# Matrix product with layer norm: another row order in the opening's row tiles, and their pieces of A loaded one by one

## The chip, the cores and the metric

The kernel runs on one core of a Trainium2 chip. The metric is the device time of one execution in microseconds; of several runs the median counts. Five engines work side by side, each with its own queue of instructions: TensorE (PE, matmuls and transposes; PEld is its loading of weights), VectorE (DVE), ScalarE (ACT), GpSimd (POOL) and SyncE (SP, which here issues most of the transfers). Sixteen DMA engines move data between the chip's memory and the on-chip buffers.

## The reference

```python
def setup_inputs():
    m, k, n = 2048, 2048, 2048
    return {
        "a": np.random.randn(m, k).astype(np.float32),
        "b": np.random.randn(k, n).astype(np.float32),
        "gamma": np.random.randn(n).astype(np.float32),
        "beta": np.random.randn(n).astype(np.float32),
        "eps": np.float32(1e-5),
    }

def reference(a, b, gamma, beta, eps):
    x = np.matmul(a, b)
    mean = np.mean(x, axis=-1, keepdims=True)
    var = np.var(x, axis=-1, keepdims=True)
    normalized = (x - mean) / np.sqrt(var + eps)
    return (gamma * normalized + beta).astype(np.float32)
```

Every row of the product is normalised by itself, so rows may be computed in any order.

## The kernel before

A, B and the output are 2048 x 2048 in float32. The rows of A are cut into 16 row tiles of 128, the contraction into 16 steps of 128 (`kt`), the columns of the output into 4 quarters of 512 (`q`). A quarter of a row tile is 16 matmuls into one PSUM bank, 1024 matmuls in all. The operands are float16: B is cast once and stays on the chip (`b16`), each row tile of A is cast and transposed, so that the contraction lies on the partitions (`at`).

Two stages follow each other.

*The opening* computes the first R = 5 row tiles together while B is still coming in, since each piece of B then serves five row tiles. A comes in column pieces of 512 (`c` = 0 to 3). For `c` = 0 each row tile's piece is a load of its own of 256 KB (`load_a1`, line 182), in the order of `arrivals` (line 163): A0, B0, A1, A2, A3, B1, B2, A4, B3. For `c` = 1 to 3 `load_pair` loads the pieces of row tiles 0 and 1, then 2 and 3, by one transfer of 512 KB each (`load_a2`, line 188) and that of row tile 4 alone (`load_a1`). All of them, and those of B (`load_b1`, `load_b2`), are issued by SP in program order, into six staging buffers (`stg`); a load waits until the casts have emptied its buffer. VectorE casts each arrived piece (lines 186, 194, 199, 205). PE transposes the pieces of A for `c` = 0 to 2 (`turn`, line 252, by hand-set spots among the matmuls) and ScalarE copies them to `at`; for `c` = 3 the transpose is a DMA (`turn_last`, line 258, in SP's queue). Until the first pieces are there, PE runs filler matmuls (line 245). The opening's parts of sums are set aside in `xs` and added up later on VectorE (`put_aside`, `add_part`, `add_rest`).

*The rest* runs row tiles 5 to 15 one after the other, with B on the chip. GpSimd loads a whole row tile with the cast in the transfer (`load_row`, line 345), and SP transposes it by DMA (`turn_ahead`, line 351), two row tiles ahead.

A row tile that is complete is normalised in two halves (`queue_norm`: `centre`, `scale`), each of which ends with one store of two quarters (`store`, line 121, issued by SP). These pieces are worked off one at a time between the quarters of later row tiles. The last row tile has an ending of its own (`finish_row`) with four stores of one quarter.

In all of this partition p of row tile i holds row 128 i + p of A and of the output.

Of the kernel before, what the change touches and what calls it, by code (L numbers as in the profile page):

```python
# [16 lines left out]
def kernel(  # L17
# [9 lines left out]
    nc = tc.nc  # L27
    P = 128
# [9 lines left out]
    KW = KC * P  # L38
    n_kc = n_kt // KC
    R = 5  # L40
# [28 lines left out]
    xs = [None] * n_mt  # L69
# [39 lines left out]
    def centre(i, q, mv):  # L109
        qs = ds(q * NB, NB)  # L110
        nc.vector.scalar_tensor_tensor(  # L111
            xs[i][:, qs], xs[i][:, qs], mv[:, 0:1], gamma_b[:, qs],
            AluOp.subtract, AluOp.mult)

    def scale(i, q, rstd):
        qs = ds(q * NB, NB)
        nc.vector.scalar_tensor_tensor(  # L117
            xs[i][:, qs], xs[i][:, qs], rstd, beta_b[:, qs],
            AluOp.mult, AluOp.add)

    def store(i, q0, nq):
        s = ds(q0 * NB, nq * NB)
        nc.sync.dma_start(out[ts(i, P), s], xs[i][:, s])

    def inv(i, sq):
        rstd = stat.tile([P, 1], FP32, tag="rstd", name=f"rstd{i}")
        nc.vector.reciprocal(rstd, sq)
        return rstd

    def queue_norm(i, mv, sq):  # L130

        got = {}

        def piece(q0):
            def run():
                centre(i, q0, mv)
                centre(i, q0 + 1, mv)
                if q0 == 0:
                    got["rstd"] = inv(i, sq)
                scale(i, q0, got["rstd"])  # L140
                scale(i, q0 + 1, got["rstd"])
                store(i, q0, 2)
            return run

        backlog.extend(piece(q) for q in range(0, n_nb, 2))

    def drain(n):
# [7 lines left out]
        out=ident, in_=ident, compare_op=AluOp.not_equal, fill=1.0,  # L155
# [7 lines left out]
    arrivals = [("a", 0), ("b", 0)] + [("a", i) for i in range(1, R - 1)]  # L163
    arrivals += [("b", 1), ("b", 2), ("a", R - 1), ("b", 3)]

    a16_of = {}
    fresh = {"st": 0}
    held = {}

    def half_stage():  # L170
        n = fresh["st"]
        if n % 2 == 0:
            held["st"] = stg.tile([P, 2, NB], FP32, tag="st", name=f"st{n // 2}")
        fresh["st"] += 1
        return held["st"][:, n % 2, :]

    def a16_room(i, c):
        if i % KC == 0:
            held["a"] = a16p.tile([P, KC, KW], FP16, tag="a16", name=f"a16s{i}_{c}")
        a16_of[i, c] = held["a"][:, i % KC, :]  # L180

    def load_a1(i, c):
        st = half_stage()
        nc.sync.dma_start(st, a[ts(i, P), ts(c, KW)])  # L184
        a16_room(i, c)
        nc.vector.tensor_copy(a16_of[i, c], st)  # L186

    def load_a2(i, c):
        st = stg.tile([P, 2, NB], FP32, tag="st", name=f"sta{i}_{c}")
        nc.sync.dma_start(  # L190
            st, a[ds(i * P, 2 * P), ts(c, KW)].rearrange("(t p) k -> p t k", p=P))
        for m in (0, 1):
            a16_room(i + m, c)
        nc.vector.tensor_copy(held["a"][:, ds(i % KC, 2), :], st)  # L194
# [6 lines left out]
    def load_b2(k, q, cast=nc.vector.tensor_copy):  # L201
        st = stg.tile([P, 2, NB], FP32, tag="st", name=f"stb{q}_{k}")
        nc.sync.dma_start(
            st, b[ds(k * P, 2 * P), ds(q * NB, NB)].rearrange("(t p) n -> p t n", p=P))
        cast(b16[:, k:k + 2, ds(q * NB, NB)], st)  # L205
        return st
# [3 lines left out]
    def load_pair(j, c):  # L210
        if len(pairs[j]) == 2:
            load_a2(pairs[j][0], c)
        else:
            load_a1(pairs[j][0], c)

    for what in arrivals:
        (load_a1(what[1], 0) if what[0] == "a" else load_b1(what[1]))
# [139 lines left out]
    for n, (k, q) in enumerate(later):  # L357
        for i in {0: (0,), 1: (1,), 2: (2,), 4: (3, 4)}.get(n, ()):
            turn_last(i)
        st = load_b2(k, q, nc.scalar.copy)  # L360
# [39 lines left out]
    def finish_row(i):  # L400
# [35 lines left out]
        rstd = inv(i, mv[:, 1:2])  # L436
        scale(i, 3, rstd)
        store(i, 3, 1)
        centre(i, 0, mv)
        for q in (1, 2):  # L440
            for h in (0, 1):
                nc.scalar.activation(  # L442
                    half(q, h), y_ps[q, h], ActFn.Copy, scale=rstd)
            store(i, q, 1)
            if q == 1:
                scale(i, 0, rstd)
                store(i, 0, 1)
# [69 lines left out]
```

## Time and profile before

| | us |
|---|---|
| median of 3 runs (lowest, highest) | 244.88 (243.92, 245.12) |
| the profiled execution, its own time | 245.38 |
| its span, first to last instruction | 242.9 |
| PE busy in the span | 234.3 |
| VectorE, ScalarE, GpSimd busy | 171.2, 65.9, 12.7 |
| matmuls of the product (line 85) busy | 223.0 |

| loads and stores | number, KB each | median us from issue to landing |
|---|---|---|
| A, one row tile's piece (`st`) | 8 x 256 | 6.5 |
| A, two row tiles' pieces (`sta`) | 6 x 512 | 6.5 |
| B, opening, one step (`st`) | 4 x 256 | 6.6 |
| B, two steps (`stb`) | 30 x 512 | 6.8 |
| stores of two quarters | 30 x 512 | 3.3 |

Times of the trace are counted from the start of the span. An engine's busy time says what it did, not what the end waited for; for that the chain of waits is read, which goes back from the last instruction to whatever released each step. The granted clock of TensorE was 0.994 over the span.

### The profile page before, as it was taken

The page shows a single profiled execution, that of the slowest core. Times are in us where ns is not written, and L with a number is a line of the kernel's source. Part 1 is how long each engine was busy: PE and PEld are TensorE (multiplying, and loading weights), DVE is VectorE, ACT ScalarE, POOL GpSimd, SP SyncE. Part 2 cuts the span into 40 slices and gives each one's busy share as a digit, 9 for nine tenths or more (in the row PEclk, how much of TensorE's full clock was granted, in tenths as well). Part 3 has the DMA queues.
Part 4 walks back from the last instruction along what each step waited for, and adds up shares of the span by engine and source line. Part 5 has one row for each costly group of instructions (what it writes and reads, how often), then busy time and mean ns, then how long its engine had stood idle before and what let it go on. Part 6 is the DMA issues. An engine that isn't in the chain of part 4 may idle for free.

```text
span 242.9 us, 2971 instructions
## 1 busy us (share of the span) xinstructions
PE 234.3 (96%) x1117; PEld 107.2 (44%) x1117; DVE 171.2 (70%) x300; ACT 65.9 (27%) x115; POOL 12.7 (5%) x20
## 2 busy tenths in 40 slices
PE   7899999999999999999999999999999999999992
PEld 2344554344444444444444444444444444444441
DVE  1543554625449998999999999998758292846761
ACT  2376444065750013020201103022111121212132
POOL 0000000000120001000000000005400000000000
PEclk9999999999999999999999999999999999999997
DMA  5999999999979999749899978988907235130405
GB/s 101 391 387 387 385 366 300 275 356 386 385 153 198 350 224 169 233 154 205 248 200 233 254 166 292 245 202 199 260 33 170 89 112 150 47 126 1 173 0 173
DMA packets 43909, 53.28 MB, mean 219 GB/s; under 512 B 27124, under 2 KB 27124, under 8 KB 43640
## 3 DMA queue, kind: packets, MB, share of 16 engines
q1 hardware_dynamic: 42312, 47.34, 62.7%
q0 software_dynamic: 1584, 5.77, 14.5%
q8 instruction: 8, 0.13, 0.2%
q14 instruction: 5, 0.04, 0.0%
HBM read 35.67 MB, written 16.78 MB: 216 GB/s over the span
## 4 chain that ended last, share of the span: by engine, by line
PE 93%; DMA 2%; DVE 1%; ACT 1%; SPq 0%; issue 0%; DVEq 0%
PE acc L85 91%; DMA st<-in_a_dram 2%; PE tps L252 1%; ACT x L442 1%; DVE x L268 1%; DVE bnst L407 0%; PE y L430 0%; DVE a16s L186 0%; PE warm L245 0%; SPq L198 0%; SPq L184 0%; PE ms_ps L425 0%; ACT mv_last L423 0%; DVE mv_last L422 0%; ACT lead L426 0%
## 5 line engine op out<-in xcount | busy, mean ns | idle before, releaser
L85 PE MATMUL acc<-b,at 128*128 128x512 f16 x1024 | 223.0, 379 | 1.5 <-DVE b L199 1.0
L85 PEld LDWEIGHTS <-at 128*128 128x128 f16 x1024 | 99.7, 98 | 120.5 <-issue 1.2
L96 DVE BATCH_NORM_STATS2 bnst<-x 128x6 f32<-128x512 f32 x43 | 29.5, 689 | 23.4 <-ACT x L95 23.4
L117 DVE SCALAR_TENSOR_TENSOR x<-x,rstd,beta_b 128x512 f32<-128x512 f32 x62 | 43.9, 748 | 0.6
L111 DVE SCALAR_TENSOR_TENSOR x<-x,mv,gamma_b 128x512 f32<-128x512 f32 x60 | 43.1, 760 | 0.0
L95 ACT COPY x<-acc 128x512 f32<-128x512 f32 x43 | 24.5, 585 | 66.9 <-PE acc L85 66.7
L272 DVE TENSOR_TENSOR x<-acc,x 128x512 f32<-128x512 f32 x20 | 13.6, 678 | 13.4 <-PE acc L85 13.4
L106 ACT ACTIVATE sq<-ve 128x1 f32<-128x1 f32 x15 | 3.0, 203 | 65.8 <-DVE ve L104 65.8
L205 DVE CAST b<-stb 128x1024 f16<-128x1024 f32 x16 | 11.1, 694 | 13.1 <-DMA stb<-in_b_dram 13.1
L205 ACT CAST b<-stb 128x1024 f16<-128x1024 f32 x14 | 14.6, 1045 | 16.6 <-DMA stb<-in_b_dram 16.6
L273 DVE BATCH_NORM_STATS2 bnst<-x 128x6 f32<-128x512 f32 x20 | 13.9, 694 | 0.7
L264 ACT COPY x<-acc 128x512 f32<-128x512 f32 x20 | 10.2, 610 | 5.7 <-PE acc L85 5.7
L254 ACT COPY at<-tps 128x512 f16<-128x512 f16 (+1 forms) x11 | 8.0, 741 | 13.1 <-PE tps L252 12.9
L345 POOL DMA_DIRECT2D a<-in_a_dram x11 | 6.0, 545 | 92.8 <-DMA at<-a 92.0
L245 PE MATMUL warm<-zeros 128*128 128x512 f16 x19 | 6.5, 476 | 1.2 <-DVE zeros L152 1.2
L186 DVE CAST a16s<-st 128x512 f16<-128x512 f32 x8 | 3.4, 428 | 5.7 <-DMA st<-in_a_dram 5.6
L194 DVE CAST a16s<-sta 128x1024 f16<-128x1024 f32 x6 | 4.2, 694 | 4.1 <-DMA sta<-in_a_dram 4.1
L391 POOL TENSOR_SCALAR gb<-gb 1x1024 f32<-1x1024 f32 x2 | 5.8, 2917 | 0.0
L252 PE MATMUL tps<-ident,a16s 128*128 128x128 f16 x60 | 5.2, 220 | 0.6 <-DVE a16s L186 0.6
L252 PEld LDWEIGHTS <-a16s 128*128 128x128 f16 x60 | 3.9, 98 | 3.9 <-DVE a16s L186 2.2
L102 DVE BATCH_NORM_AGGREGATE mv<-bnst 128x2 f32<-128x24 f32 x15 | 4.0, 264 | 0.5
L245 PEld LDWEIGHTS <-zeros 128*128 128x128 f16 x19 | 2.1, 118 | 4.4 <-issue 2.9
(33 smaller groups left out, 26.3 us busy)
## 6 DMA issues: line engine op xcount, KB each, us to landing
stb<-in_b_dram SPq DMA_DIRECT2D x30, 512.0 KB, 6.8
out_dram<-x SPq DMA_DIRECT2D x30, 512.0 KB, 3.3
a<-in_a_dram POOLq DMA_DIRECT2D x11, 512.0 KB, 6.2
sta<-in_a_dram SPq DMA_DIRECT2D x6, 512.0 KB, 6.5
st<-in_a_dram SPq DMA_DIRECT2D x8, 256.0 KB, 6.5
st<-in_b_dram SPq DMA_DIRECT2D x4, 256.0 KB, 6.6
gamma_b<-in_gamma_dram SPq DMA_DIRECT2D x1, 1024.0 KB, 5.5
beta_b<-in_beta_dram SPq DMA_DIRECT2D x1, 1024.0 KB, 8.3
```

The costliest lines, as they stand in the source:

```text
L85: nc.tensor.matmul(acc[i, q], at(i)[:, kt, :], b16[:, kt, ds(q * NB, NB)], start=first, stop=last,)
L95: nc.scalar.copy(xs[i][:, qs], acc[i, q])
L96: nc.vector.bn_stats(bnst[i][:, q, :], xs[i][:, qs])
L111: nc.vector.scalar_tensor_tensor(xs[i][:, qs], xs[i][:, qs], mv[:, 0:1], gamma_b[:, qs], AluOp.subtract, AluOp.mult)
L117: nc.vector.scalar_tensor_tensor(xs[i][:, qs], xs[i][:, qs], rstd, beta_b[:, qs], AluOp.mult, AluOp.add)
L205: cast(b16[:, k:k + 2, ds(q * NB, NB)], st)
L245: nc.tensor.matmul(warm if to is None else to, zeros[:, 0:P], zeros, start=True, stop=True)
L252: nc.tensor.transpose(t_ps[:, m, j, :], a16_of[i, c][:, ts(j, P)], ident)
L254: nc.scalar.copy(pair[i0 // 2][:, ds(i0 % 2, n), ds(c * KC, KC), :], t_ps)
L264: nc.scalar.copy(xs[p][:, ds(q * NB, NB)], acc.pop((p, q)))
L272: nc.vector.tensor_tensor(xs[p][:, qs], acc[p, q], xs[p][:, qs], AluOp.add)
L273: nc.vector.bn_stats(bnst[p][:, q, :], xs[p][:, qs])
```

## The change

Row tiles 0 to 4 keep their 128 rows, but these lie on the partitions in another order: partition 8e + j holds row e + 16j (e from 0 to 15, j from 0 to 7). The new function `spread` is this view of a row tile in memory. The loads of A in the opening (`load_a1`, `load_a2`) read through it and the stores of row tiles 0 to 4 write through it, so that each row ends up where it belongs. B and row tiles 5 to 15 keep their order.

`load_a2` issues two transfers of 256 KB, one for each row tile, in place of one of 512 KB; the cast behind them is still one for both. Row tile 0 is stored by four transfers of one quarter in place of two of two quarters.

```diff
     def store(i, q0, nq):
         s = ds(q0 * NB, nq * NB)
-        nc.sync.dma_start(out[ts(i, P), s], xs[i][:, s])
+        nc.sync.dma_start(spread(out, i, s) if i < R else out[ts(i, P), s], xs[i][:, s])
...
                 scale(i, q0 + 1, got["rstd"])
-                store(i, q0, 2)
+                for q, nq in ((q0, 1), (q0 + 1, 1)) if i == 0 else ((q0, 2),):
+                    store(i, q, nq)
...
+    def spread(x, i, cols):
+        return x[ts(i, P), cols].rearrange("(j e) n -> e j n", e=16)
...
     def load_a1(i, c):
         st = half_stage()
-        nc.sync.dma_start(st, a[ts(i, P), ts(c, KW)])
+        nc.sync.dma_start(st, spread(a, i, ts(c, KW)))
...
     def load_a2(i, c):
         st = stg.tile([P, 2, NB], FP32, tag="st", name=f"sta{i}_{c}")
-        nc.sync.dma_start(
-            st, a[ds(i * P, 2 * P), ts(c, KW)].rearrange("(t p) k -> p t k", p=P))
+        for m in (0, 1):
+            nc.sync.dma_start(st[:, m, :], spread(a, i + m, ts(c, KW)))
```

## The prediction

> **What bounds the kernel now.** I read the chain that ended last first, then the busy times, then the opening by stretches of time, then the two queues that the change touches. The page's chain of waits (section 4: shares of the span by engine, then by line):
>
> ```profile
> PE 93%; DMA 2%; DVE 1%; ACT 1%; SPq 0%; issue 0%; DVEq 0%
> ```
>
> Nine tenths of the span is one unbroken run of matmuls (line 85). The same chain in order of time (start us, duration us, what) shows where it is not PE:
>
> ```profile
> 1.66 6.00 DMA st<-in_a_dram
> 7.66 0.02 issue
> 7.69 0.44 DVE a16s L186
> ...
> 12.31 12.73 PE acc L85 x59
> ...
> 48.17 185.79 PE acc L85 x860
> ```
>
> From 1.66 to 7.66 us the end is set by a load of A (row tile 1, column piece 0). From 12.31 on PE never waits for a load; its one pause, around 47 us, is for PSUM banks that VectorE empties. So the change can move the end in two ways: let the first tiles land at another time, or make a later piece of A so late that PE waits for it. The opening by stretches (start:end and length in us, then busy us and counts of PE, PEld, DVE, ACT, POOL, the granted clock, the DMA engines' busy share, GB/s):
>
> ```profile
> 0.00:3.00 3.00, 1.81 (x5) 0.71 (x6) 0.35 (x2) 1.28 (x1) 0.49 (x5) 1.00 0.22 70
> 3.00:6.00 3.00, 2.44 (x12) 0.91 (x11) 0.43 (x1) 0.16 (x1) 0.00 (x0) 1.00 0.80 126
> 6.00:9.00 3.00, 1.87 (x14) 0.68 (x12) 1.28 (x3) 0.82 (x2) 0.00 (x0) 1.00 1.05 395
> ...
> 12.00:36.00 24.00, 24.00 (x146) 12.15 (x145) 11.41 (x18) 13.24 (x22) 0.00 (x0) 1.00 1.05 384
> 36.00:48.00 12.00, 11.73 (x54) 5.15 (x53) 6.36 (x10) 2.54 (x5) 0.00 (x0) 1.00 1.08 282
> ```
>
> This is the table to look at twice. Between 3 and 6 us the sixteen DMA engines are 80% busy and move 126 GB/s; from 6 us on, just as busy, they move 385 to 395. Whatever they do in the ramp, it is not moving bytes at their pace, though five loads had been issued by then. Last, VectorE's casts (start us, duration us, engine, line, operation; in brackets the idle time before and what ended it), which give the arrival of each piece:
>
> ```profile
> 4.92 0.43 DVE L186 CAST a16s<-st 128x512 f16<-128x512 f32 x1 [3.71 <-DMA st<-in_a_dram]
> 7.01 0.43 DVE L199 CAST b<-st 128x512 f16<-128x512 f32 x1 [1.67 <-DMA st<-in_b_dram]
> 7.69 0.43 DVE L186 CAST a16s<-st 128x512 f16<-128x512 f32 x1 [0.25 <-DMA st<-in_a_dram]
> 8.36 0.43 DVE L186 CAST a16s<-st 128x512 f16<-128x512 f32 x1 [0.25 <-DMA st<-in_a_dram]
> ```
>
> The first piece of B lands 2.09 us after the first of A (7.01 - 4.92); every later 256 KB piece lands 0.67 to 0.68 us after the one before. 0.68 us for 262,144 B is 386 GB/s, the pace of the full stream.
>
> **The change, part by part.**
>
> 1. *The matmuls, transposes, casts and statistics* keep their number and shapes: the row order inside a row tile is only a name for a partition, and rows 0 to 4 are stored back through the same view. Cost 0.
>
> 2. *Two loads for one in `load_a2`*, six times. On SP each extra issue costs 0.46 us (three of line 184 back to back take 1.37 us; line 190 alone takes 0.37), 6 x 0.46 = 2.8 us of SP. It lies beside the stream: a piece of A lands a median 6.5 us after its issue because it queues behind others, and from 11.5 to 36 us SP issues loads of 0.37 us about every 1.4 us and otherwise waits for staging room. If that cover were gone, the second half of each pair, and behind it the next load of B in SP's order, would be 0.46 us late, and the cast in line 194 with it. On the DMA engines the split costs what the cadence shows: 256 KB pieces come every 0.68 us, 512 KB pieces (casts at 17.14, 18.50, 19.85) every 1.36; 2 x 0.68 - 1.36 = 0. The cast now needs two landings; one more semaphore step of 0.017 us (what such a step takes on SP before line 203) x 6 = 0.1 us on VectorE, which stands idle 0.67 us before each of these casts. Queued behind that cast on VectorE are the next casts of B, and PE waits for those only if they lose more than the slack given below. I take the middle, 0.05 us; bounds 0 and 0.1. [...]
>
> 3. *Row 0 stored by four transfers instead of two.* Two more issues of about 0.4 us on SP near 97 us. SP waits 103.4 us in all there for VectorE (line 117), up to 10.2 at once, and behind these stores stands one transpose of A at 107.74 for a row tile that PE reaches later. Cost 0; without that idle time 0.8 us for this transpose.
>
> 4. *The stores of rows 0 to 4 through the view.* Today ten transfers, median 3.3 us to landing, from 97 to about 130 us, while PE runs its 185.79 us without a wait and the last store is row 15's, which is not touched. Cost 0, with over 80 us of cover.
>
> 5. *The order in which A's rows are read*, the only part with a price. No row shows a read in the new order, so I bound it. Best end: the ramp goes away. From 3 to 6 us (388 - 126) x 3.00 = 786 KB were not moved (388 GB/s is the rate from 12 to 15 us in a finer table), and 786 KB at 388 GB/s is 2.03 us. Every us of it moves A1's landing at 7.66, and with it the whole chain, since behind it PE and the load stream shift together. Gain at most 2.03 us. Worst end: the new order is read more slowly than the stream. The nearest row of a slower stream is 282 GB/s (36 to 48 us, where other work shares the engines): 0.93 us a piece instead of 0.68, worked out below to 2.8 us of loss. Between them I take the share of the ramp that is A's: of the six loads issued first (A0, B0, A1, A2, A3, B1) four are A's, 4/6 x 2.03 = 1.35 us. I lean to the gain because the steady stream already runs with all engines out of step and at its pace, so the new order has little to lose there, whereas the ramp, where all engines begin together at rows a fixed distance apart, is the place where the order can matter.
>
> [...]
>
> Sum: -1.35 + 0.05 = -1.3 us. The profiled execution took 245.38 us (span 242.9 and 2.5 around it), 0.5 over the median of the runs, 244.88. It would take 244.1, the median 243.6.
>
> **The rivals.**
>
> *A. The order does not matter: 244.9 us.* The ramp is then the engines' or the memory's way of starting, whatever is read. For it: the ramp hits B0 as well (its cast begins at 7.01), which is read as before. The steady stream cannot gain: at 384 to 395 GB/s A and B come at one pace. Against it: the DMA engines count as busy in the ramp. The same time follows if the new view is turned into the same reads.
>
> *B. The new order is slower than the stream: about 246.9 us.* Each engine then steps 128 KB from row to row instead of 8 KB if the view is cut as its name says. Place: the transposes of row tiles 2 and 3, third column piece. Their cast runs from 30.20 to 30.89, PE begins them at 31.63: a slack of 0.74 us, the smallest in the opening. Up to there 14 pieces of A (5 + 5 + 4) have come through a stream without gaps, so this decides from 0.74 / 14 = 0.053 us a piece, 8% slower. At 282 GB/s it is 14 x 0.254 - 0.74 = 2.8 us; halfway between there and a loss just over 1.2 us, 2.0. For it: the stream has no gaps from 6 to 36 us, so every lost ns adds up. Against it: between 12 and 36 us loads of A and of B, in single rows or in pairs of rows 1 MB apart, come at one and the same pace, so the stream there seems not to ask in what order rows are read.
>
> **How the numbers follow.** This kernel's runs lie 0.5% apart, so 0.5% (1.22 us) is about what can be told from no change: 243.66 to 246.10 is "same". The forecast (a gain from 0.3 to 2.0 us) gets 0.52, of which 0.38 is over 1.22 us and 0.14 under. Rival A gets 0.18, all within. Rival B gets 0.30, of which 0.27 is over 1.22 us. Faster 0.38, same 0.14 + 0.18 + 0.03 = 0.35, slower 0.27. The range begins at 242.6 (the whole ramp, 2.03, and 0.25 of scatter) and goes into rival B up to 246.6, leaving out some 0.15 there and 0.04 below. The forecast's own range is 242.6 to 244.6.
>
> **What would show it.** The forecast holds if the cast of B0 begins before 6.5 us, that of A1 before 6.8, and the stretch from 3 to 6 us moves well over 126 GB/s, with 384 GB/s kept from 12 to 36 us. Rival A: the same arrival times within 0.2 us. Rival B: casts of single pieces of A more than 0.73 us apart, and PE waiting for line 194 near 31 us. Parts 2 to 4 are wrong if PE waits for a cast while 384 GB/s still hold, or if the transposes of A after 97 us come late. The prediction as a whole fails if the ramp gets longer, for B0 too: then the order matters with the other sign.

## The result and the profile after

The changed kernel takes 255.66 us (median of 6 runs, 253.73 to 256.76) against 244.61 us before (6 runs). The ratio is 1.0458, 95% interval 1.0426 to 1.049: slower by some 11 us, where 1.3 us of gain was forecast. The profiled execution was the fastest of the six, 253.73 us with a span of 251.8; a second one (e15_again) took 254.52 with 252.5.

The opening by the same stretches of time as before (start:end, length, busy us of PE, PEld, DVE, ACT, POOL, granted clock, busy share of the DMA engines, GB/s):

```profile
0.00:3.00 3.00, 1.81 (x5) 0.71 (x6) 0.35 (x2) 1.28 (x1) 0.50 (x5) 1.00 0.19 44
3.00:6.00 3.00, 2.68 (x11) 0.95 (x10) 0.43 (x1) 0.00 (x0) 0.00 (x0) 1.00 0.74 160
6.00:9.00 3.00, 2.57 (x13) 0.80 (x10) 1.20 (x3) 0.95 (x2) 0.00 (x0) 1.00 1.09 296
...
12.00:36.00 24.00, 21.11 (x120) 10.09 (x117) 8.92 (x14) 11.84 (x20) 0.00 (x0) 1.00 1.06 312
```

The ramp is hardly touched (160 GB/s instead of 126). What broke is the stream behind it: from 12 to 36 us the engines are as busy as before (1.06 against 1.05) and move 312 GB/s instead of 384, and PE, which had been busy all 24 us, is busy for 21.11. Engines as busy that move less mean slower transfers, not fewer: where almost only A arrives, a packet of 2 KB takes 125 ns instead of 84 (median, below). VectorE's casts in the changed kernel (start us, duration us, then the idle time before and its end) show whose:

```profile
6.70 0.43 DVE L205 CAST b<-st 128x512 f16<-128x512 f32 x1 [1.22 <-DMA st<-in_b_dram]
7.72 0.43 DVE L192 CAST a16s<-st 128x512 f16<-128x512 f32 x1 [0.59 <-DMA st<-in_a_dram]
8.65 0.43 DVE L192 CAST a16s<-st 128x512 f16<-128x512 f32 x1 [0.51 <-DMA st<-in_a_dram]
9.59 0.43 DVE L192 CAST a16s<-st 128x512 f16<-128x512 f32 x1 [0.51 <-DMA st<-in_a_dram]
10.30 0.43 DVE L205 CAST b<-st 128x512 f16<-128x512 f32 x1 [0.28 <-DMA st<-in_b_dram]
```

Pieces of A now come 0.93 and 0.94 us apart, where it was 0.68; the piece of B behind them takes 0.71. Here, where almost only A arrives, it is what is read through the new view that is slow; farther on B is slowed beside it (e5_wide and the packets, below). PE's timeline shows the first place where that is felt, and it is not where a piece of A is transposed:

```profile
25.81 0.61 PE L258 MATMUL tps<-ident,a16s 128*128 128x128 f16 x8
27.56 1.02 PE L85 MATMUL acc<-b,at 128*128 128x512 f16 x4 [1.15 <-DVE b L211]
...
35.01 1.24 PE L85 MATMUL acc<-b,at 128*128 128x512 f16 x5 [1.37 <-DVE b L211]
```

PE waits for a cast of B (line 211), whose load is natural but stands behind slow pieces of A in SP's queue and moves beside them. Over the whole span (engine, line, what it waited for: us in total, times, longest):

```profile
PE acc L85 <- DVE b L211: 4.3, 5, 1.4
...
PE acc L85 <- DVE x L274: 1.3, 2, 1.1
...
PEld L258 <- DVE a16s L200: 1.1, 1, 1.1
...
PE tps L258 <- DVE a16s L200: 0.6, 1, 0.6
```

The second line is PE waiting near 55 us for PSUM banks, which VectorE empties later because its casts are late; before the change that wait was 0.4 us in all.

The start times of the same matmul of line 85 in both traces, counted from 0 for the first one, tell where the loss arises better than the chain of waits:

```
matmul     before   after   later by
10          11.71   12.29    0.58
69          24.67   25.59    0.92
70          25.33   27.56    2.23
100         33.59   38.90    5.31
140         42.22   48.35    6.13
180         51.62   59.55    7.93
383         95.44  103.36    7.92
384         95.66  104.09    8.43
1022       233.36  241.81    8.45
```

All but half a us is lost before 60 us. (The 0.5 us at matmul 384, the first of row tile 6, is a late DMA transpose of A; in the second profile it is 0.26 us, and the delay in the opening 8.8. It does not come from the stores through the view: e4_step16, with natural stores, has 1.5 us of it, and e8_stores, with the view in the stores alone, none.) The chain itself is a trap here. After the change it reads:

```profile
PE 56%; issue 29%; DMA 9%; SPq 3%; DVE 1%; ACT 0%; POOL 0%; POOLq 0%
```

It is followed back from the last instruction, enters by that small wait at matmul 384 the transposes in SP's queue and then GpSimd's load, and leaves out the whole opening as 70.90 us of "issue". A chain shows one way back; the 8 us lie beside it.

### The profile page after: what moved, and what is told of

Same layout as the page of the kernel before. It is cut to its first block, busy times and chain, and to the rows that moved or that the text cites. A ratio compares the mean times of both kernels' runs of the same rounds, so it can differ in the third digit from the quotient of the medians.

```text
span 251.8 us, 2989 instructions
## 1 busy us (share of the span) xinstructions
PE 237.3 (94%) x1117; PEld 107.5 (43%) x1117; DVE 171.2 (68%) x300; ACT 66.1 (26%) x115; POOL 12.9 (5%) x20
## 4 chain that ended last, share of the span: by engine, by line
PE 56%; issue 29%; DMA 9%; SPq 3%; DVE 1%; ACT 0%; POOL 0%; POOLq 0%
PE acc L85 55%; DMA at<-a 6%; DMA a<-in_a_dram 3%; SPq L377 2%; PE y L436 1%; SPq L357 1%; SPq L394 0%; DVE bnst L413 0%; ACT x L448 0%; SPq L378 0%; PE ms_ps L431 0%; ACT mv_last L429 0%; POOL ident L155 0%; DVE mv_last L428 0%; DVE zeros L153 0%
## 5 line engine op out<-in xcount | busy, mean ns | idle before, releaser
L251 PE MATMUL warm<-zeros 128*128 128x512 f16 x19 | 7.4, 534 | 1.2 <-DVE zeros L153 1.2
```

The costliest lines, as they stand in the source:

```text
L251: nc.tensor.matmul(warm if to is None else to, zeros[:, 0:P], zeros, start=True, stop=True)
```

## The experiments

Fourteen other kernels were run, and the changed one a second time, each beside the kernel before. Ratios are to the kernel before, with their 95% interval.

**e1_split: the splits without the view.**

```diff
     def spread(x, i, cols):
-        return x[ts(i, P), cols].rearrange("(j e) n -> e j n", e=16)
+        return x[ts(i, P), cols]
```

> The changed kernel with its two splits kept (load_a2 as two transfers, row 0 stored by four) but the rows in their natural order, in loads and stores. Theory 'view' (the loss comes from how the new view is read): 244.6 us as before, within 0.5%, single pieces of A 0.68 us apart. Rival 'split' (the loss comes from the additional transfers, which take semaphore slots and SP time): about 255 us, as the changed kernel.

Measured: 244.55 us, ratio 0.9995 (0.9974 to 1.0015). The additional transfers cost nothing that can be seen, to some 0.6 us either way; what is left is the view.

**e2_blocks, e3_step5, e4_step16: the order of rows, or the form of the view?** Three views that name other rows. The first has two steps as the changed kernel's has, but its blocks are neighbouring rows; the others have a single step.

```diff
-        return x[ts(i, P), cols].rearrange("(j e) n -> e j n", e=16)
+        return x[0:R * P, cols].rearrange("(e m j) n -> m e j n", e=16, m=R)[i]
```
```diff
-        return x[ts(i, P), cols].rearrange("(j e) n -> e j n", e=16)
+        return x[0:R * P, cols].rearrange("(p m) n -> m p n", m=R)[i]
```
```diff
-        return x[ts(i, P), cols].rearrange("(j e) n -> e j n", e=16)
+        return x[:, cols].rearrange("(p m) n -> m p n", m=n_mt)[i]
...
-        nc.sync.dma_start(spread(out, i, s) if i < R else out[ts(i, P), s], xs[i][:, s])
+        nc.sync.dma_start(out[ts(i, P), s], xs[i][:, s])
```

> The changed kernel with another two-step view: row tile i of the opening holds rows 40e + 8i + j, so that each block of eight partitions reads eight neighbouring rows, 8 KB apart, as in the natural order; only the view still has two steps (16 blocks of 8). Theory 'memory order' (rows 128 KB apart within a block are slow to read): about 245 us, pieces of A 0.68 us apart. Rival 'form' (any view of 16 times 8 is slow to move, whatever rows it names): about 255 us, pieces 0.94 us apart.

> The changed kernel with a one-step view that also reorders rows: row tile i of the opening holds rows i + 5p, 40 KB from partition to partition. Rival 'form': 244.6 us, since the view has one step of 128; pieces of A 0.68 us apart. Theory 'memory order': slower than before if the distance of 40 KB is slow, up to 255.

> One step of 128 again, with rows i + 16p of A in the opening, 128 KB from partition to partition, as far apart as the rows of one block in the changed kernel. The output rows of the opening are stored in natural places and hold other rows' results; the work is the same. Theory 'memory order': about 255 us and pieces 0.94 us apart. Rival 'form': 245 us and 0.68 us.

Measured: e2_blocks 256.53 us, 1.0487 (1.0413 to 1.0561); e3_step5 244.65, 1.0014 (0.9991 to 1.0037); e4_step16 245.66, 1.0033 (1.0003 to 1.0063). The same stretch, 12 to 36 us, first in e2_blocks:

```profile
12.00:36.00 24.00, 20.88 (x121) 10.18 (x121) 9.19 (x14) 11.84 (x20) 0.00 (x0) 1.00 1.06 316
```

and in e3_step5:

```profile
12.00:36.00 24.00, 24.00 (x146) 12.14 (x145) 12.16 (x19) 13.24 (x22) 0.00 (x0) 1.00 1.05 387
```

Neighbouring rows through a two-step view are slow (316 GB/s); rows 40 KB apart through a one-step view are not (387), and rows 128 KB apart, as far as within the changed kernel's blocks, aren't either (385 GB/s in e4_step16). In these orders, up to 128 KB from row to row, the order in memory plays no part in the stream (384 GB/s in the natural one). "Memory order" fell, "form" stood.

**e5_wide: a price per row or per byte?**

```diff
-        for m in (0, 1):
-            nc.sync.dma_start(st[:, m, :], spread(a, i + m, ts(c, KW)))
+        nc.sync.dma_start(
+            st.rearrange("p t k -> p (t k)"), spread(a, i, ds((c - 1) * KW, 2 * KW)))
```

> The changed kernel, but each pair's two transfers (128 rows x 2 KB of two row tiles) are one transfer of 128 rows x 4 KB of one row tile through the same view; the bytes per staging buffer are the same, the columns are other ones, so the opening's sums are of other data. Theory 'per row' (each row read through a two-step view costs a fixed extra, 0.94 - 0.68 = 0.26 us per 128 rows): 6 x 0.26 = 1.6 us less than the changed kernel, pairs 1.62 us apart instead of 1.88. Theory 'per row, hidden' (the rows are handed out at 0.94 us per 128, which 4 KB rows hide): pairs 1.36 us apart, 6 x 0.52 = 3.1 us less. [...]

Measured: 255.11 us, 1.0441 (1.038 to 1.0503). The casts of two successive pairs of A (line 200) and of the B between them (line 211):

```profile
21.02 0.69 DVE L200 CAST a16s<-sta 128x1024 f16<-128x1024 f32 x1 [1.24 <-DMA sta<-in_a_dram]
22.89 0.69 DVE L211 CAST b<-stb 128x1024 f16<-128x1024 f32 x1 [1.18 <-DMA stb<-in_b_dram]
24.77 0.69 DVE L200 CAST a16s<-sta 128x1024 f16<-128x1024 f32 x1 [1.19 <-DMA sta<-in_a_dram]
```

They begin 1.87 and 1.88 us apart. Twice the bytes per row cost twice the time (274 ns a packet of 4 KB, in the table further down, against 125 of 2 KB): the extra is per byte, and both forms of "per row" fell. The B in the middle is as large as a pair and read by one step, and it takes 1.87 us as well, where 512 KB took 1.36 before. So a slow load also slows what moves beside it.

**e6_halves and e7_evens: does it matter which partitions a transfer writes?** Natural rows again, one step, 64 partitions a transfer: neighbouring ones, or every other one (the pairs likewise).

```diff
-        nc.sync.dma_start(st, spread(a, i, ts(c, KW)))
+        for h in (0, 1):
+            nc.sync.dma_start(st[ts(h, 64), :], a[ds(i * P + h * 64, 64), ts(c, KW)])
```
```diff
-            nc.sync.dma_start(st[ts(h, 64), :], a[ds(i * P + h * 64, 64), ts(c, KW)])
+            nc.sync.dma_start(st[ds(h, 64, 2), :], a[ds(i * P + h, 64, 2), ts(c, KW)])
```

> Rows in natural order, each piece of A loaded by two transfers of 64 neighbouring partitions (0 to 63, 64 to 127), one step each. [...] Theory 'per row': natural one-step reads, 0.68 us a piece, 245 to 247 us; if 64 rows are handed out like the two-step view, 0.94 us and about 255.

> As e6_halves, but the two transfers are the even and the odd partitions (rows to match). [...] Theory 'per row': the same as e6_halves within 1%.

Measured: e6_halves 257.45 us, 1.0537 (1.0471 to 1.0603); e7_evens 252.03, 1.0315 (1.0248 to 1.0383). From 6 to 12 us in e6_halves:

```profile
6.00:12.00 6.00, 4.00 (x25) 1.63 (x24) 2.56 (x6) 2.05 (x4) 0.00 (x0) 1.00 1.05 276
```

and in e7_evens:

```profile
6.00:12.00 6.00, 3.70 (x24) 1.55 (x23) 2.13 (x5) 1.95 (x4) 0.00 (x0) 1.00 0.82 246
```

These two look alike in GB/s and are different things. In e6_halves the engines are fully busy (1.05) and slow; in e7_evens they stand idle a fifth of the time (0.82), because SP, at about 0.6 us for each of 40 transfers, does not feed them; most of their packets go at full pace (84 ns in the table of packets further down). In e6_halves the casts of A are 0.97 to 1.02 us apart. 'Per row' had the two kernels within 1% of each other; they lie 2.1% apart, and the place on the partitions matters.

**e8_stores: only the stores through the view.**

```diff
-        nc.sync.dma_start(st, spread(a, i, ts(c, KW)))
+        nc.sync.dma_start(st, a[ts(i, P), ts(c, KW)])
...
-            nc.sync.dma_start(st[:, m, :], spread(a, i + m, ts(c, KW)))
+            nc.sync.dma_start(st[:, m, :], a[ts(i + m, P), ts(c, KW)])
```

> The changed kernel with the loads of A in natural order, so that only the stores of row tiles 0 to 4 go through the view (their rows come out permuted). If the loads alone make the loss: 244.6 us within 0.5%. If the stores have a share (transposes of A waiting behind them in SP's queue, seen around 104 us in the changed kernel): 1 to 3 us slower than before.

Measured: 244.11 us, 0.9994 (0.9972 to 1.0016). The loads alone make the loss; the stores cost nothing that can be seen, to some 0.6 us either way.

**e9_evens_wide, e10_narrow, e11_grouped, e12_spread_evens: rows of another length, transfers in another order, a two-step view by every other partition.** e9 takes the pairs as even and odd partitions with 4 KB rows, all else natural; e10 takes the changed kernel's view in two transfers of 1 KB rows; e11 exchanges the two loops of e6_halves' pairs; e12 takes the changed kernel's row order by even and odd partitions.

```diff
+        flat = st.rearrange("p t k -> p (t k)")
+        for h in (0, 1):
+            nc.sync.dma_start(
+                flat[ds(h, 64, 2), :], a[ds(i * P + h, 64, 2), ds((c - 1) * KW, 2 * KW)])
```
```diff
+        for h in (0, 1):
+            nc.sync.dma_start(
+                st[:, ts(h, 256)], spread(a, i, ds(c * KW + h * 256, 256)))
```
```diff
-        for m in (0, 1):
-            for h in (0, 1):
+        for h in (0, 1):
+            for m in (0, 1):
```
```diff
+        for h in (0, 1):
+            nc.sync.dma_start(st[ds(h, 64, 2), :], spread(a, i, ts(c, KW))[:, ds(h, 4, 2), :])
```

> Rows in natural order. Pairs of A's pieces loaded as even and odd partitions of one row tile with 4 KB rows (two transfers of 64 rows; other columns than before, so the opening's sums are of other data); single pieces by one step over 128 partitions, as before the change. [...] Rival 'step' (a step of two partitions is what frees the transfer): pairs 1.36 us apart, within 1% of before.

> The changed kernel's view, but each piece of A by two transfers of 256 columns, 1 KB a row. [...] Rivals 'per row' and 'form': 40 transfers of 128 rows at 0.94 us each, far over 260 us.

> e6_halves with the four transfers of a pair in another order: both row tiles' lower 64 partitions, then both upper. [...] If the place does not matter: as e6_halves (257.5) within 1%.

> The changed kernel's row order, loaded by even and odd partitions (views of 16 times 4). [...] Rival 'form' (any view of two steps is slow): 255 us or more, with the engines busy at 300 GB/s.

Measured: e9 244.63 us, 1.0045 (1.0016 to 1.0075); e10 259.86, 1.0647 (1.0576 to 1.0718); e11 258.96, 1.061 (1.0523 to 1.0697); e12 256.3, 1.0501 (1.0361 to 1.0641). From 12 to 36 us in e9_evens_wide:

```profile
12.00:36.00 24.00, 24.00 (x143) 12.03 (x142) 11.96 (x18) 13.21 (x23) 0.00 (x0) 1.00 1.05 391
```

and in e12_spread_evens:

```profile
12.00:36.00 24.00, 21.45 (x120) 9.95 (x118) 9.18 (x16) 11.84 (x20) 0.00 (x0) 1.00 0.95 288
```

The length of a row does not decide. e9 has rows of 4 KB in its pairs, as e5_wide has, and goes at full pace (391 GB/s, 165 ns a packet against 274), within 1% of before, as rival 'step' had it; e10 has rows of 1 KB and is slow (266 GB/s in the same stretch), though not as slow as its rivals' "far over 260 us". Nor is every other partition enough: e12, which takes them through a two-step view, has engines as busy as e7_evens in that stretch (0.95 against 0.96) and moves 288 GB/s instead of 324, and its 256.3 us lie over the 255 that 'form' had as the least. e11 is slower than e6_halves by 1.5 us (0.6%), with intervals that overlap: undecided.

**e13_own and e14_shared: is a two-step view slow as such?** Each transfer has eight blocks: of four neighbouring partitions (e13, four transfers of 32 partitions a piece) or of eight (e14, two transfers of 64). The stores keep the natural order, so that the rows come out permuted. With W = 32 and W = 64:

```diff
-        nc.sync.dma_start(st, spread(a, i, ts(c, KW)))
+        for g in range(P // W):
+            nc.sync.dma_start(
+                st[ts(g, W), :],
+                a[ds(i * P + g * W, W), ts(c, KW)].rearrange("(j e) n -> e j n", e=8))
```

> [...] Slow as a whole, since SP has 80 transfers to issue. [...] Rival 'form' (a two-step view is slow whatever its blocks): about 126 ns.

> [...] Rival 'form': 126 ns here and in e13_own alike. [...]

Measured, one execution each: 280.17 and 264.75 us beside 244.21. The times don't answer the question: SP has 80 or 40 such transfers to issue, and for each of them the trace has nine updates of the semaphore, one a little over 1 us after the issue and eight as it lands, where a load of B has sixteen (the author's reading, which no record confirms: eight engines work on it instead of sixteen). From 12 to 36 us the engines of e13_own are busy for two thirds:

```profile
12.00:36.00 24.00, 18.52 (x82) 7.85 (x83) 6.72 (x12) 9.39 (x18) 0.00 (x0) 0.86 0.65 207
```

The answer lies in the single packets. In these transfers a packet is one row: the loads of the opening and the four stores of one quarter have 11264 rows of 2 KB before the change, and the trace has 11264 packets of 2 KB. It records each packet's duration. Counted from 12 to 42 us, A and B together:

```
kernel            packet   median   upper quartile   over 100 ns per 2 KB
before              2 KB    86 ns       91 ns           3%
after               2 KB    99         128             48%
e6_halves           2 KB    99         131             49%
e11_grouped         2 KB    96         152             48%
e7_evens            2 KB    84          84              6%
e12_spread_evens    2 KB    84         105             27%
e13_own             2 KB    84          84             11%
e14_shared          2 KB    88         124             32%
e5_wide             4 KB   274         296             86%
e9_evens_wide       4 KB   165         167              3%
```

B's packets, though read by one step, are not spared. In e10_narrow A comes in packets of 1 KB, so that every packet of 2 KB is B's: from 17 to 36 us their median is 131 ns and 76% are over 100 ns, against 86 ns and 1% for all packets in the kernel before. In the changed kernel 1902 of 2704 packets are over 100 ns in that stretch, in which at most ten pieces of A, 1280 packets, move; from 14 to 17 us, when only B arrives, none of 565 is.

In the changed kernel from 6.2 to 9.3 us, when almost only A arrives, the median is 125 ns against 84 before: 1.5 times. e13_own reads through two-step views and keeps 84 ns, so "form" as such fell, as far as one execution shows it; e14_shared, whose eight blocks are twice as long, has three times as many slow packets (32% against 11%). Its upper quartile of 124 ns is near the 126 that 'form' had; its median of 88 is not. Its engines, too, are idle for a sixth of the time (0.84 busy from 12 to 36 us).

**e15_again: a second profile of the changed kernel.**

> The changed kernel once more, for a second profiled execution: the first one was the fastest of its six runs (253.73 us, median 255.66). If the whole loss comes from late pieces in the opening, the matmuls are about as late at 60 us as at the end; if a later wait (row tile 6's transpose, 0.5 us in the first profile) grows in slower runs, the delay grows after 100 us.

Measured: 254.52 us. Its matmuls are 8.79 us late at matmul 180 and 9.06 at the end: the opening again. Neither profile shows the 1 to 2 us by which the median of six runs lies higher still; where these arise stays open. (The profiled execution before was itself 0.8 us above its median, 245.38 against 244.61, so the first pair of profiles shows 8.4 of the 11 us.)

## Why the prediction was wrong

*What bounds the kernel* was read rightly: PE, with a load of A at the start, and a later piece of A as the one other way to move the end. That second way is what happened, but PE waited mostly for pieces of B, behind and beside those of A.

*Parts 1 to 4* hold. The splits and the stores through the view cost nothing that can be seen (e1_split 0.9995, e8_stores 0.9994, each to about 0.2%); the longer list of stores for row 0 is in both. One price within them was off without consequence: an issue through the view takes SP 0.54 to 0.70 us, not 0.46.

*Part 5 is the step that failed.* Of the two ends, a gain of 2.03 us from the ramp and a loss from a slower stream, it chose the gain, by the reason that "the steady stream already runs with all engines out of step and at its pace, so the new order has little to lose there". (Before the change the sixteen updates of the load that lands at 18.48 us, in the steady stream, are spread over 1.23 us; those of the first load of the ramp, 2.86 to 4.90, over 2.04, so that there too the parts of a load land far apart.) That reason looked at the order of rows only. The runs show that the order indeed has nothing to lose (e3_step5, e4_step16) and nothing that lasts to gain: in e3 the first matmul starts at 6.39 us instead of 7.49, but e1_split, in natural order, has 7.01, and by matmul 20 e3 is level with before. So the other half of the reason failed too, that every us of the ramp moves the whole chain. What the part did not price is that the view changes the *form* of the transfer, from one step of 128 partitions to 16 steps of 8, and no row of the trace had such a load. Its bound from the nearest slow row, 282 GB/s or 0.93 us a piece, met the measured 0.93 to 0.94, but by luck: in that row DMA transposes stand among the loads (line 258, from 38.76 us on), and no load has two steps. The pace of the bad end was there; the choice between the ends was wrong, and so was the price of the bad end, 2.8 us (rival B).

*Rival B* was the right case with the wrong cause (rows 128 KB apart, which e4_step16 reads at 385 GB/s) and too small a price, 2.0 to 2.8 us against 7.9 to 8.8 in the opening. Both of its signs came: pieces 0.93 us apart, and a wait of PE for the cast of a pair of A (line 200 now), though at 36.9 us and after a longer one for B. Its threshold (0.053 us a piece) was passed fivefold by 0.26. Its price counted only 14 pieces, to one place, less a slack of 0.74 us called "the smallest in the opening". It was not. Before the change VectorE and PE show, for a piece of B:

```profile
24.10 0.69 DVE L205 CAST b<-stb 128x1024 f16<-128x1024 f32 x1 [2.20 <-DMA stb<-in_b_dram]
25.33 1.03 PE L85 MATMUL acc<-b,at 128*128 128x512 f16 x4
```

The cast ends at 24.79 and PE uses it at 25.33, a slack of 0.54, and PE did stop there, at matmul 70. And six more pieces follow: 20 x 0.26 = 5.2 us, before any slack is taken off. The runs show three things more that the price left out. B's own pieces are slow beside A's (131 ns a packet in e10_narrow, 1.87 us for 512 KB in e5_wide). PE waits 0.9 us longer for PSUM banks behind VectorE's late casts. And a piece counts as landed with the last of the sixteen updates of its semaphore (before the change at 7.66 us for row tile 1's first piece, whose cast begins at 7.69). In both kernels the last update falls behind the others near 24 to 27 us (1.7 us behind the fifteenth before, 1.4 after); before, it is 0.4 behind at 39 us, after the change 2.2 at 45. How the remaining 2.7 to 3.6 us divide is not settled.

*Rival A* had the memory side right: the order of rows costs nothing in e3_step5 and e4_step16, with 387 and 385 GB/s at 40 and 128 KB from row to row, against 384 before at 8 KB. It could not see what the form of a transfer does, and its time, 244.9, would have been that of e3_step5 (244.65).

*What makes the two-step view slow* is not shown, since no record says which engine writes which partition. What is shown: one step over all 128 partitions, in each of the three row orders tried, or over every other one, goes at 84 to 87 ns a row of 2 KB (medians); 64 neighbouring partitions do not (49% of the packets over 100 ns in e6_halves, against 6% for every other one in e7_evens); two steps of 16 times 8 do not (125 ns where almost only A arrives); two steps of 8 times 4 do (84 ns in e13_own, one execution, its engines idle for a third of the time). And the slowness is not a price that a load pays for its own form alone, since B's one-step loads pay it beside such a load (131 ns in e10_narrow, against 86 before). Whether the transfers hinder each other at the memory or at the buffer was not shown: in e6_halves and e7_evens the rows read go with the partitions written. That row orders cost nothing makes the memory the less likely place; that is the author's estimate.

## What to carry to other kernels

A view that reorders rows should keep the partitions as one step: `(p m) n -> m p n` reorders rows at no cost that could be measured, `(j e) n -> e j n` with 16 blocks of 8 cost half as much again per byte loaded (125 ns a packet instead of 84), and slowed the one-step loads beside it. Before a stream that fills the DMA engines is touched, look at the form of each transfer and not only at its bytes and addresses, and price a slow piece as pieces times its extra, less the smallest slack of anything behind it in the queue, whatever tensor it belongs to; the pieces of other tensors that move beside it count too. When the DMA engines are equally busy and move less (1.05 and 276 GB/s in e6_halves from 6 to 12 us), look at the packets; when they are less busy (0.82 and 246 in e7_evens), look at who issues.

## What had not been expected of the hardware

- A load of the same bytes through 16 steps of 8 partitions: 125 ns per 2 KB packet instead of 84, and 274 instead of 165 per 4 KB; a store through the same view costs the kernel nothing (0.9994).
- A load by one step of 128 partitions that moves beside such loads is slowed too: B's 2 KB packets at 131 ns (e10_narrow, 17 to 36 us).
- Transfers of 64 partitions are at full pace when these are every other one (84 ns; with 4 KB rows 165 ns, and the kernel at 1.0045) and slow when they are neighbours (upper quartile 131 ns).
- The ramp from 3 to 6 us moves 126 to 240 GB/s, with engines that are 71 to 90% busy, in the ten kernels whose ramp was read, whatever the rows: it seems to belong to the start. In these the first matmul falls between 6.2 and 7.7 us, without any visible effect on the end where the stream behind it keeps its pace.
